# Hybrid decoder step on one core: a credit of 3 for each piece of the sample's state, the memory cache through other tiles, memory values in strips, and another order of the first loads

## The chip, the cores and the metric

One Trainium2 chip, one core. The metric is the device time of one execution in microseconds (us); lower is better. The profile names the engines PE (TensorE, the matrix engine), ACT (ScalarE), DVE (VectorE), POOL (GpSimd) and SP (SyncE, which here only issues transfers). POOL and ACT can issue transfers too. Each engine works through its own instructions in their order.

## The reference

One layer of a decoder for 256 tokens of a prompt and 8 tokens of a sample, all in float32, width 2048:

```python
h = rmsnorm(x); q, k, v, z, xbc, dt, qm, g = split(h @ w_in)
A = sliding-window attention (window 128, ALiBi, sinks; 16 query heads, 4 key heads of 64)
B = Mamba-2 SSD (32 heads of 64, state 128; conv of 4; y * silu(z), group RMSNorm)
M = cross-attention of 4 heads of 256 into 256 memory tokens
x = x + w_out(sig(g0) * w_up_swa(A) + sig(g1) * w_up_ssd(B) + sig(g2) * w_up_mem(M))
x = x + w_down(silu(rmsnorm(x) @ w_gate) * (rmsnorm(x) @ w_up))
```

For the prompt, the memory's keys and values are rmsnorm(mem_prompt) @ w_mem_kv. For each of the 8 sample tokens they come from a cache (`cache_mem_k`, `cache_mem_v`: 256 tokens of 4 heads of 256), and the SSD state comes from `state_ssm` (8 tokens, 32 heads, 64 x 128) and is updated and written out: state = state * decay + B * (dt * x), y = sum(state * C).

## The kernel before

**Weights.** All weight matrices are cut into "units" of 256 x 512 float32 (512 KB), some 610 of them in a fixed order: memory keys and values (units 0 to 31, `pmem`), the input projection (`pin`: memory queries, queries, keys, gates, B, C, dt, x and z by groups), the branch products (`pua` for A, `pum` for M, `pus` for B), `pout`, and the feed-forward part (`pg`, `pu`, `pdn`). SP loads a unit into `raw` four units ahead. ACT writes a rounded copy `hi`, DVE writes the rest `lo = raw - hi` (`split`), three units ahead. PE then does 24 products of 264 columns per unit (12 of 512 in the memory stage): high by high, high by low, low by high. Gate groups of branch B (units 250 to 281) end with unit 281, and the first `pus` is unit 282.

**Side work.** Everything else is written as generators in two lists, `side` and `slow`. After each unit, `step` gives the first of them a credit (1.0 and 0.75, at most 3.0 saved); a generator runs until its yields have spent the credit. The number after `yield` therefore sets how many units pass before the next piece. `drain(name)` runs a task to its end at once. A scheduler then puts the written instructions into each engine's order; it keeps what depends on what and may move the rest.

**The slow list.** `mem_sample_work` (task Mk) multiplies cached keys with queries on DVE (`jks`), `mem_sample_values` (Ms) multiplies the softmax weights with the cached values on PE (`oms`, in strips of 32 rows of the result), then `ssd_sample_work` (Y0 to Y3) updates the state in 32 pieces of 4 tokens and 2 heads: ACT scales (`ring` at L1294), DVE adds and sums (L1295, L1296), POOL writes out. Last comes `ssd_sample_end` (task end): PE sums squares (`ssys`), DVE takes a reciprocal root (L171 to L176) and multiplies (L1316, L1318), ACT and DVE split the result into `sT`, which is an input of every `pus`. `slow.drain("end")` stands in `before_ups(0)`, ahead of unit 282.

**Loads.** `ahead(sources, pool, depth)` issues loads on POOL's queue, `depth` of them before they are used. Tiles come from `lm` (two tiles of 512 KB) or from `ring`, a buffer of two such pieces that is used round and round. The first loads are on SP: memory rows in quarters (`load_mem`), two gain vectors (`vg`), and the first units. PE turns `vg` (`pv`) and the memory rows (`memT`); ACT scales these into `memh` (L316), and the squares of the rows (L327) give their norm.

Of the kernel before, what the change touches and what calls it, by code (L numbers as in the profile page):

```python
# [77 lines left out]
def tile_hybrid_decoder_step(  # L78
# [80 lines left out]
    def mm(out, lhsT, rhs, start=True, stop=True):  # L159
        nc.tensor.matmul(out, lhsT=lhsT, rhs=rhs, start=start, stop=stop)  # L160
# [18 lines left out]
    def split(hi, lo, src):  # L179

        act(hi, src, AF.Copy)  # L181
        V.tensor_tensor(lo, src, hi.bitcast(F32), op=ALU.subtract)  # L182

# [18 lines left out]

    for t in range(2):
        load_mem(t, 0, 0)
    nc.sync.dma_start(vg[0:16], norm_mem[0].rearrange("(c p) -> c p", p=P))
    nc.sync.dma_start(vg[16:32], norm_mix[0].rearrange("(c p) -> c p", p=P))
# [45 lines left out]
    def do_split(n):  # L252
        if n < state["split"]:
            return
        raw = raws.pop(n)
        hi = wp.tile([P, 1024], F32R, tag="hi", name=nm("hi"), bufs=3)
        lo = wp.tile([P, 1024], F32R, tag="lo", name=nm("lo"), bufs=3)
        if units[n].get("perm"):
            for k in range(2):
                v = [t[:, k * 512:(k + 1) * 512].rearrange("p (r a d) -> p a r d", r=4, a=2) for t in (hi, lo)]  # L260
                s = raw[:, k * 512:(k + 1) * 512].rearrange("p (a r d) -> p a r d", a=2, r=4)
                split(v[0], v[1], s)
        else:
            split(hi, lo, raw)
        parts[n] = (hi, lo)
        state["split"] = n + 1
# [53 lines left out]
    def mem_norm():  # L320
        junk = t2("junk", BF16)
        ssm_ = tiny("ssm", 16)
        for h in range(2):
            for t in range(2):
                for c in range(4):
                    o = 8 * t + 4 * h + c
                    act(junk[:, 0:256], mem_t[t, h][:, c * 256:(c + 1) * 256], AF.Square, accum_out=ssm_[:, o:o + 1])  # L327
                yield 1.3
# [9 lines left out]
    def mem_group(cg):  # L338
        st = {}

        def prod(u):
            def f(hi, lo):
                if u == 0:
                    st["ps"] = [dps("pmem") for _ in range(2)]
                if cg == 0:
                    for f in ((0, 1, 2) if u == 0 else (u + 2,)):
# [72 lines left out]
    def prep_x():  # L419
# [4 lines left out]
        for h in range(2):  # L424
            for t in range(2):
# [3 lines left out]
                yield 1.3  # L429
# [165 lines left out]
    mem_loads = ahead([(None, c[0, b, mc * P:(mc + 1) * P].rearrange("m h d -> m (h d)"))  # L595
                       for c in (cache_mem_k, cache_mem_v) for b in range(NS) for mc in range(2)], lm, 2)
# [97 lines left out]
    def mem_sample_work():  # L694
# [3 lines left out]
        for b in range(NS):  # L698
            qb = t4("qb")[:, 0:1024]
            nc.gpsimd.dma_start(qb, qd[b:b + 1].broadcast_to([P, 1024]))  # L700
            for mc in range(2):
                kc = next(mem_loads)
# [23 lines left out]
    def mem_sample_values():  # L726
        pT = mT["p"]
# [12 lines left out]
        o = t1("omsb")[:, 0:256]  # L740
        V.tensor_copy(o, po[:, 0:256])
        ps = sps("omT")
        for d in range(2):
            tr(ps[:, d * P:(d + 1) * P], o[:, d * P:(d + 1) * P])
        o = tiny("omsT", 64)
        V.tensor_copy(o.rearrange("p (h d b) -> p d h b", h=4, d=2),
                      ps[:, 0:256].rearrange("p (d h e) -> p d h e", d=2, h=4)[:, :, :, 0:NS])
# [73 lines left out]
    def swa():  # L821
# [37 lines left out]
        for a in range(2):  # L859
# [6 lines left out]
            yield 1.0  # L866
        qst = [half("qst", F32R) for _ in range(2)]
        for kvp in range(2):
            for a in range(2):
# [5 lines left out]
                yield 0.8  # L875
        for blk in (1, 0):
            nk = 256 if blk else 128
            for kvp in range(2):
# [38 lines left out]
                for rp in range(2):  # L917
                    for kb in range(nk // P):
# [12 lines left out]
                        yield 0.4  # L931
# [348 lines left out]
    def ssd_sample_work(g):  # L1280
# [5 lines left out]
        for j in range(4 * g, 4 * g + 4):  # L1286
# [3 lines left out]
            for b0 in (0, 4):  # L1290
# [7 lines left out]
                yield 2.0  # L1298
# [313 lines left out]
    side.add("x", prep_x())  # L1612
# [63 lines left out]
```

## Time and profile before

| | us |
|---|---|
| median of 3 runs | 1930.85 |
| lowest and highest of them | 1927.42, 1932.12 |
| the profiled execution, device time | 1933.54 |
| its span, first to last instruction | 1931.8 |

| engine | busy us | share of the span |
|---|---|---|
| PE | 1905.2 | 99 % |
| DVE | 1168.0 | 60 % |
| ACT | 969.7 | 50 % |
| POOL | 133.6 | 7 % |

The mean granted clock of PE is 0.999. In the profile a line such as L1294 is a line of the kernel's source; names left and right of the arrow are the tiles that an instruction writes and reads, with buffer numbers left out. In a timeline, a bracket at the end gives the idle time of the engine before the instruction and what ended it; an x8 merges eight of the same kind.

### The profile page before, as it was taken

What the parts mean: (1) busy time and instruction counts of PE and PEld (TensorE: products, weight loads), DVE (VectorE), ACT (ScalarE), POOL (GpSimd) and SP (SyncE); (2) the same over time, 40 slices, a digit from 0 to 9 for tenths busy, and PEclk for the clock granted to TensorE, in tenths of its full rate; (3) what the DMA queues carried; (4) which work ended last, traced back from release to release, by engine and by line L of the source; (5) the groups of instructions that cost most, each with busy time, mean ns of one, the idle gap of its engine ahead of it and who ended that gap; (6) DMA issues with size and microseconds to landing.
All of it is one profiled execution on the core that took longest, in us unless ns stands there. A gap on an engine that the chain in (4) does not pass through costs nothing.

```text
span 1931.8 us, 37682 instructions
## 1 busy us (share of the span) xinstructions
PE 1905.2 (99%) x15401; PEld 1857.1 (96%) x15401; DVE 1168.0 (60%) x2246; ACT 969.7 (50%) x1423; POOL 133.6 (7%) x269
## 2 busy tenths in 40 slices
PE   8999999999999999999999999999999999999998
PEld 6899999989999999999999999999999999999998
DVE  5665577665568878588455666555445555445553
ACT  6654456665657685646444444444334434334443
POOL 3010101001002122011000000000000000000000
PEclk9999999999999999999999999999999999999999
DMA  8686758767668789778656656665556665566653
GB/s 278 209 264 214 212 171 297 223 190 234 200 181 279 241 228 301 250 262 282 180 189 213 222 182 176 184 182 180 183 178 183 178 185 177 184 177 183 176 192 126
DMA packets 191956, 402.92 MB, mean 209 GB/s; under 512 B 13891, under 2 KB 16242, under 8 KB 191648
## 3 DMA queue, kind: packets, MB, share of 16 engines
q1 hardware_dynamic: 169856, 324.13, 54.6%
q0 software_dynamic: 21776, 76.33, 11.9%
q8 instruction: 120, 1.97, 0.4%
q14 instruction: 52, 0.43, 0.1%
q10 hardware_dynamic: 152, 0.07, 0.0%
HBM read 376.53 MB, written 26.22 MB: 208 GB/s over the span
## 4 chain that ended last, share of the span: by engine, by line
PE 87%; DMA 4%; issue 4%; DVE 3%; ACT 2%; POOL 1%; ACTq 0%; SPq 0%; POOLq 0%; DVEq 0%
PE pin L160 25%; PE pu L160 13%; PE pdn L160 13%; PE pg L160 13%; PE pus L160 5%; PE pout L160 5%; PE pmem L160 5%; DMA ring<-in_state_ssm_dram 2%; PE pum L160 1%; PE pua L160 1%; DVE lo L182 1%; DMA ld<-in_cache_mem_v_dram 1%; DVE ring L1295 1%; DMA ld<-in_cache_mem_k_dram 1%; ACT hi L181 0%
## 5 line engine op out<-in xcount | busy, mean ns | idle before, releaser
L182 DVE TENSOR_TENSOR lo<-raw,hi 128x1024 fp32r<-128x1024 f32 (+1 forms) x626 | 746.8, 1196 | 599.4 <-ACT hi L181 598.2
L181 ACT ACTIVATE hi<-raw 128x1024 fp32r<-128x1024 f32 (+1 forms) x626 | 646.0, 1036 | 835.0 <-PE pin L160 191.8
L160 PE MATMUL pin<-hh,hi 128*128 128x264 f32 x1728 | 489.3, 287 | 0.6 <-DVE sig L1439 0.5
L160 PE MATMUL pin<-hl,hi 128*128 128x264 f32 x1728 | 489.0, 286 | 0.0
L160 PE MATMUL pin<-hh,lo 128*128 128x264 f32 x1728 | 473.8, 285 | 1.8 <-DVE lo L182 1.8
L160 PEld LDWEIGHTS pin<-hh,hi 128*128 128x128 f32 x1728 | 325.4, 189 | 5.6 <-issue 3.6
L160 PEld LDWEIGHTS pin<-hl,hi 128*128 128x128 f32 x1728 | 325.5, 188 | 2.7 <-issue 2.4
L160 PEld LDWEIGHTS pin<-hh,lo 128*128 128x128 f32 x1728 | 317.3, 188 | 3.8 <-DVE lo L182 2.3
L160 PE MATMUL pdn<-fah,hi 128*128 128x264 f32 x704 | 199.7, 285 | 0.0
L160 PE MATMUL pdn<-fal,hi 128*128 128x264 f32 x704 | 199.4, 285 | 0.0
L160 PE MATMUL pu<-h2h,hi 128*128 128x264 f32 x704 | 199.4, 284 | 0.0
L160 PE MATMUL pu<-h2l,hi 128*128 128x264 f32 x704 | 199.3, 284 | 0.0
L160 PE MATMUL pg<-h2l,hi 128*128 128x264 f32 x704 | 199.1, 285 | 0.0
L160 PE MATMUL pg<-h2h,hi 128*128 128x264 f32 x704 | 198.4, 284 | 0.0
L160 PE MATMUL pdn<-fah,lo 128*128 128x264 f32 x704 | 197.0, 284 | 0.0
L160 PE MATMUL pu<-h2h,lo 128*128 128x264 f32 x704 | 196.6, 284 | 0.0
L160 PE MATMUL pg<-h2h,lo 128*128 128x264 f32 x704 | 196.1, 284 | 0.0
L160 PEld LDWEIGHTS pdn<-fah,hi 128*128 128x128 f32 x704 | 132.7, 189 | 0.1
L160 PEld LDWEIGHTS pu<-h2h,hi 128*128 128x128 f32 x704 | 132.7, 189 | 0.0
L160 PEld LDWEIGHTS pg<-h2h,hi 128*128 128x128 f32 x704 | 132.7, 188 | 0.0
L160 PEld LDWEIGHTS pdn<-fal,hi 128*128 128x128 f32 x704 | 132.6, 188 | 0.1
L160 PEld LDWEIGHTS pu<-h2l,hi 128*128 128x128 f32 x704 | 132.6, 188 | 0.0
(531 smaller groups left out, 2966.0 us busy)
## 6 DMA issues: line engine op xcount, KB each, us to landing
raw<-in_w_in_dram SPq DMA_DIRECT2D x218, 512.0 KB, 4.3
raw<-in_w_gate_dram SPq DMA_DIRECT2D x88, 512.0 KB, 3.7
raw<-in_w_up_dram SPq DMA_DIRECT2D x88, 512.0 KB, 3.9
raw<-in_w_down_dram SPq DMA_DIRECT2D x88, 512.0 KB, 4.2
raw<-in_w_mem_kv_dram SPq DMA_DIRECT2D x32, 512.0 KB, 4.5
raw<-in_w_up_ssd_dram SPq DMA_DIRECT2D x32, 512.0 KB, 4.2
raw<-in_w_out_dram SPq DMA_DIRECT2D x32, 512.0 KB, 4.4
ld<-in_cache_mem_k_dram POOLq DMA_DIRECT2D x16, 512.0 KB, 5.8
```

Of the source, the lines that this page charges most:

```text
L160: nc.tensor.matmul(out, lhsT=lhsT, rhs=rhs, start=start, stop=stop)
L181: act(hi, src, AF.Copy)
L182: V.tensor_tensor(lo, src, hi.bitcast(F32), op=ALU.subtract)
L1295: V.scalar_tensor_tensor(hb, bb[:, b], dx[:, b:b + 1], hb, op0=ALU.mult, op1=ALU.add)
```

## The change

It has these parts.
1. The two gain loads go from SP's queue to ACT's, ahead of the memory rows. The squares of the memory rows are placed behind ACT's first split. Feature chunks of the memory rows are turned one unit ahead instead of two.
2. The loads of x wait until unit 7 is written, and spend less credit; the sliding-window steps spend less too.
3. The cached keys come through four tiles (`lm` and `ring` in turn), the cached values through `lm` apart from them.
4. The values are multiplied in strips of 32 x 512, four for each token, from one zeroed table of weights; parts are added at the end by four reductions after four transposes.
5. A state piece spends 3.0 instead of 2.0 of credit.

```diff
@@ mem rows, gains
+    nc.scalar.dma_start(vg[0:16], norm_mem[0].rearrange("(c p) -> c p", p=P))
+    nc.scalar.dma_start(vg[16:32], norm_mix[0].rearrange("(c p) -> c p", p=P))
     for t in range(2):
         load_mem(t, 0, 0)
-    nc.sync.dma_start(vg[0:16], norm_mem[0].rearrange("(c p) -> c p", p=P))
-    nc.sync.dma_start(vg[16:32], norm_mix[0].rearrange("(c p) -> c p", p=P))
...
@@ do_split: the first split is kept
-            split(hi, lo, raw)
+            h = split(hi, lo, raw)
+            if n == 0:
+                state["first"] = h
...
@@ mem_norm
-                    act(junk[:, 0:256], mem_t[t, h][:, c * 256:(c + 1) * 256], AF.Square, accum_out=ssm_[:, o:o + 1])
+                    with tc.issue_after(state["first"].ins):
+                        act(junk[:, 0:256], mem_t[t, h][:, c * 256:(c + 1) * 256], AF.Square, accum_out=ssm_[:, o:o + 1])
...
@@ memory units
-                    for f in ((0, 1, 2) if u == 0 else (u + 2,)):
+                    for f in ((0, 1) if u == 0 else (u + 1,)):
...
@@ prep_x, loads of x
-                yield 1.3
+                yield 0.4
...
@@ loads of the caches
-    mem_loads = ahead([(None, c[0, b, mc * P:(mc + 1) * P].rearrange("m h d -> m (h d)"))
-                       for c in (cache_mem_k, cache_mem_v) for b in range(NS) for mc in range(2)], lm, 2)
+    homes = [0]
+
+    def anywhere(name):
+        homes[0] += 1
+        return (lm if homes[0] % 2 else ld)(name)
+
+    memk_loads, memv_loads = (
+        ahead([(None, c[0, b, mc * P:(mc + 1) * P].rearrange("m h d -> m (h d)")) for b in range(NS) for mc in range(2)],
+              pool, depth) for c, pool, depth in ((cache_mem_k, anywhere, 4), (cache_mem_v, lm, 2)))
...
@@ mem_sample_values
-            w = t1("pb")[:, 0:256].rearrange("p (mc h e) -> p mc h e", mc=2, h=4)
-            V.memset(w.rearrange("p mc h e -> p (mc h e)"), 0.0)
-            V.tensor_copy(w[:, :, :, b], pT.rearrange("p (mc b h) -> p mc b h", mc=2, b=NS)[:, :, b])
-            for mc in range(2):
-                vc = next(mem_loads)
-                for h in range(4):
-                    mm(po[32 * h:32 * h + 32, 0:256], w[:, mc, h], vc[:, h * 256:(h + 1) * 256],
-                       start=b == 0 and mc == 0, stop=b == NS - 1 and mc == 1)
-                yield 1.5
...
+        w = t2("pb").rearrange("p (mc b c) -> p mc b c", mc=2, b=NS)
+        V.memset(w.rearrange("p mc b c -> p (mc b c)"), 0.0)
+        for b in range(NS):
+            V.tensor_copy(w[:, :, b, 4 * b:4 * b + 4], pT[:, :, b])
...
+            vc = [next(memv_loads) for _ in range(2)]
+
+            for mc, e in ((1, 0), (1, 1), (0, 0), (0, 1)):
+                o = 64 * mc + 32 * e
+                tc.keep_in_program_order(mm(po[o:o + 32, 0:512], w[:, mc, b], vc[mc][:, 512 * e:512 * e + 512],
+                                            start=b == 0, stop=b == NS - 1))
+            yield 3.0
+        o = t2("omsb")
+        V.tensor_copy(o, po)
...
+        for j in range(4):
+            tr(ps[:, j * P:(j + 1) * P], o[:, j * P:(j + 1) * P])
...
+        for h in range(4):
+            V.tensor_reduce(o.rearrange("p (h d b) -> p h d b", h=4, d=2)[:, h], v[:, h % 2, h // 2, h], axis=AX.X, op=ALU.add)
...
@@ swa_keys, swa: three yields
-            yield 1.0
+            yield 0.3
-                yield 0.8
+                yield 0.3
-                        yield 0.4
+                        yield 0.2
...
@@ ssd_sample_work
-                yield 2.0
+                yield 3.0
...
@@ end of the kernel
-    side.add("x", prep_x())
+    side.add("x", prep_x(), ["go"])
...
         if i == 7:
             side.drain("m")
+            side.ready.add("go")
```

How it moves instructions is shown at three places. First, POOL at the start of the program, before: `knm_bc`, `sink`, `kn_bc`, `dtb_bc` and `na_bc` are small vectors that are copied to all 128 partitions, `vb` and `va` are vectors loaded as rows.

```order
L330 DMA knm_bc<-in_k_norm_mem_dram 128x256
L496 DMA sink<-in_swa_sinks_dram 128x16
masks.py:199 ISA
masks.py:199 AFFINE_SELECT ident<-ident 128x128 [waits Pool_49]
L497 DMA kn_bc<-in_k_norm_swa_dram 128x64
L498 DMA dtb_bc<-in_dt_bias_dram 128x32
L499 DMA na_bc<-in_a_log_dram 128x32
L501 DMA hcol<-in_dt_bias_dram 32x1
L501 DMA hcol<-in_a_log_dram 32x1
L501 DMA hcol<-in_d_skip_dram 32x1
L502 AFFINE_SELECT tri<-ones 128x128 [waits Pool_49]
L513 MEMSET slope 128x1
```

And after:

```order
L221 DMA vb_84<-in_conv_b_dram 24x128
L221 DMA vb_84<-in_ssd_norm_dram 16x128
masks.py:199 ISA
masks.py:199 AFFINE_SELECT ident<-ident 128x128 [waits Pool_49]
L221 DMA vb_84<-in_norm_ffn_dram 16x128
L221 DMA vb_84<-in_q_norm_mem_dram 2x128
L223 DMA vb_84<-in_q_norm_swa_dram 1x16x4 x2
L224 DMA va_83<-in_conv_w_dram 96x128
L334 DMA knm_bc<-in_k_norm_mem_dram 128x256
L500 DMA sink<-in_swa_sinks_dram 128x16 [waits DMASW0_49]
L501 DMA kn_bc<-in_k_norm_swa_dram 128x64 [waits DMASW1_49]
L502 DMA dtb_bc<-in_dt_bias_dram 128x32 [waits DMASW2_49]
```

The rows of `vb` and `va`, seven loads, have moved ahead of the copies to all partitions. On SP, the same place before:

```order
L201 DMA ring<-in_mem_prompt_dram 128x512
L201 DMA mem_87<-in_mem_prompt_dram 128x512
L205 DMA vg_85<-in_norm_mem_dram 16x128
L206 DMA vg_85<-in_norm_mix_dram 16x128
L244 DMA raw_143<-in_w_mem_kv_dram 128x2x512
L201 DMA ring<-in_mem_prompt_dram 128x512
```

And after, where the two `vg` rows stand on ACT's queue and the first `raw` is third:

```order
L202 DMA ring<-in_mem_prompt_dram 128x512
L202 DMA mem_89<-in_mem_prompt_dram 128x512
L245 DMA raw_143<-in_w_mem_kv_dram 128x2x512
L202 DMA ring<-in_mem_prompt_dram 128x512
L202 DMA mem_89<-in_mem_prompt_dram 128x512
L245 DMA raw_145<-in_w_mem_kv_dram 128x2x512
```

Second, PE at the first of the value products (`oms`, read from the cached tiles `ld`), before:

```order
L160 MATMUL ps_4193<-kst_3119,qst_3209 128x128 x8
L160 MATMUL oms_4150<-ld_4255,pb_4343 32x256 x4
L160 MATMUL pin_4269<-hl_115,hi_4315 128x264
L160 MATMUL pin_4269<-hh_113,lo_4316 128x264
L160 MATMUL pin_4269<-hh_113,hi_4315 128x264
L160 MATMUL pin_4269<-hl_115,hi_4315 128x264
L160 MATMUL pin_4269<-hh_113,lo_4316 128x264
L160 MATMUL pin_4270<-hh_113,hi_4315 128x264
L160 MATMUL pin_4270<-hl_115,hi_4315 128x264
L160 MATMUL pin_4270<-hh_113,lo_4316 128x264
L160 MATMUL oms_4150<-ld_4346,pb_4343 32x256 x4
L160 MATMUL pin_4270<-hh_113,hi_4315 128x264
```

And after:

```order
L160 MATMUL pin_4347<-hh_113,lo_4464 128x264
L160 MATMUL pin_4348<-hh_113,hi_4463 128x264
L160 MATMUL oms_4214<-ld_4217,pb_4204 32x512 x2
L160 MATMUL oms_4214<-ld_4215,pb_4204 32x512 x2
L164 MATMUL pT_4256<-ident,s_4000 128x128 x2
L164 MATMUL pT_4256<-ident,s_4001 128x128 x2
L160 MATMUL pin_4348<-hl_115,hi_4463 128x264
L160 MATMUL pin_4348<-hh_113,lo_4464 128x264
```

Two groups of four products of 256 columns, some rows apart, stand there before; one group of four products of 512 columns is there now.

Third, PE at the first `pus` (unit 282), before:

```order
L160 MATMUL pin_11404<-hh_113,hi_11521 128x264
L160 MATMUL pin_11404<-hl_115,hi_11521 128x264
L160 MATMUL pin_11404<-hh_113,lo_11522 128x264
L160 MATMUL pus_11652<-sT_6539,hi_11551 128x264 [waits Activation_49]
L160 MATMUL pus_11652<-sT_6539,hi_11551 128x264
L160 MATMUL pus_11652<-sT_6539,lo_11552 128x264 [waits DVE_49]
```

And after:

```order
L160 MATMUL pin_11258<-hh_113,hi_11392 128x264
L160 MATMUL pin_11258<-hl_115,hi_11392 128x264
L160 MATMUL pin_11258<-hh_113,lo_11393 128x264
L160 MATMUL ssys_11571<-ys_1559_11569,ones 128x32 [waits PE_49]
L160 MATMUL pus_11603<-sT_6301,hi_11422 128x264 [waits Activation_49]
L160 MATMUL pus_11604<-sT_6301,hi_11422 128x264
L160 MATMUL pus_11605<-sT_6301,hi_11422 128x264
```

Before, `ssys` stands nineteen units of products earlier; now it is the row just ahead of the first `pus`, which waits for ACT's `sT`. DVE's rows that lead from `ssys` to `sT` there, after the change:

```order
L182 TENSOR_TENSOR lo_11466<-raw_11420,hi_11465 128x1024 [waits DMAHW6_49,PE_49,Activation_49]
L1330 TENSOR_SCALAR vys_11573<-ssys_11571 128x32 [waits PE_49]
L171 TENSOR_SCALAR rs_y_11575<-vys_11573 128x32 [waits DVE_49]
L172 TENSOR_SCALAR rs_y_11575<-rs_y_11575 128x32 [waits DVE_49]
L174 TENSOR_TENSOR rs_a_11576<-rs_y_11575 128x32 [waits DVE_49]
L182 TENSOR_TENSOR lo_11496<-raw_11463,hi_11495 128x1024 [waits DMAHW7_49,Activation_49]
L175 SCALAR_TENSOR_TENSOR rs_a_11576<-rs_a_11576,vys_11573 128x32 [waits DVE_49]
L176 SCALAR_TENSOR_TENSOR rs_y_11575<-rs_a_11576,rs_y_11575 128x32 [waits DVE_49]
L174 TENSOR_TENSOR rs_a_11576<-rs_y_11575 128x32 [waits DVE_49]
L175 SCALAR_TENSOR_TENSOR rs_a_11576<-rs_a_11576,vys_11573 128x32 [waits DVE_49]
L176 SCALAR_TENSOR_TENSOR rs_y_11575<-rs_a_11576,rs_y_11575 128x32 [waits DVE_49]
L174 TENSOR_TENSOR rs_a_11576<-rs_y_11575 128x32 [waits DVE_49]
```

Before, the same rows stand at the place of `ssys`, nineteen units ahead of the first `pus`; now one `lo` is left among them, and `sT` is read right behind.

More of the change, by code (lines that the diff above doesn't have):

```diff
@@ L159, in mm @@
     def mm(out, lhsT, rhs, start=True, stop=True):
-        nc.tensor.matmul(out, lhsT=lhsT, rhs=rhs, start=start, stop=stop)
+        return nc.tensor.matmul(out, lhsT=lhsT, rhs=rhs, start=start, stop=stop)
     def tr(out, in_):
@@ L179, in split @@
     def split(hi, lo, src):
-        act(hi, src, AF.Copy)
+        h = act(hi, src, AF.Copy)
         V.tensor_tensor(lo, src, hi.bitcast(F32), op=ALU.subtract)
+        return h
     ident = const([P, P], "ident")
@@ L701, in mem_sample_work @@
             for mc in range(2):
-                kc = next(mem_loads)
+                kc = next(memk_loads)
                 jk = t1("jks")
```

9 lines of the change are left out of this document (2 added, 7 removed).

## The prediction

> **What bounds the kernel now.** I read the page's first part, then the busy time by stage, then TensorE's waits, then the timeline around each wait.
>
> ```profile
> PE 1905.2 (99%) x15401; PEld 1857.1 (96%) x15401; DVE 1168.0 (60%) x2246; ACT 969.7 (50%) x1423; POOL 133.6 (7%) x269
> 560.00:760.00 200.00, 192.72 (x1669) 188.65 (x1668) 166.52 (x492) 135.67 (x233) 43.26 (x61) 0.99 0.83 249
> 760.00:876.00 116.00, 115.87 (x1001) 114.71 (x1000) 82.76 (x162) 67.38 (x100) 19.00 (x31) 1.00 0.81 275
> 876.00:1932.00 1056.00, 1050.79 (x8624) 1050.05 (x8623) 565.82 (x777) 441.90 (x511) 8.33 (x13) 1.00 0.60 186
> PE pua L160 <- ACT sig L1434: 3.8, 2, 2.6
> PE pmT L164 <- DVE pm L674: 1.7, 2, 1.3
> ```
>
> The first row is the whole span; the next three are stretches (length, then each engine's busy time and count, TensorE's granted clock, DMA share and GB/s); the last two are waits of TensorE (total us, times, longest). TensorE is busy for 99 % of the 1931.8 us. From 760 us on there is next to nothing to take: 116.00 less 115.87 us idle, and 1056.00 less 1050.79, spread over 8624 matmuls and the end. A gain can come from the start (until the first product, below), from the waits, from 560 to 760 us, where 200.00 less 192.72 leaves 7.3 us idle, and from matmuls that fall away. A loss can come from any new wait of TensorE, above all in the clean part. 0.3 % of the time, 5.8 us, is about what a measurement of this kernel can tell from no change.
>
> **Start: gain loads off SP's queue, POOL's loads in another order.**
>
> ```profile
> 1.73 0.42 SPq L205 DMA_DIRECT2D vg<-in_norm_mem_dram  x1
> 2.66 0.42 SPq L244 DMA_DIRECT2D raw<-in_w_mem_kv_dram  x1
> 1.41 0.72 POOL L330 DMA_DIRECT2D knm_bc<-in_k_norm_mem_dram  x1 [0.25 <-issue]
> 6.91 0.55 POOL L220 DMA_DIRECT2D vb<-in_conv_b_dram  x1 [0.38 <-DMA knm_bc<-in_k_norm_mem_dram]
> 2.00:4.00 2.00, 0.00 (x0) 0.00 (x0) 0.17 (x1) 0.10 (x1) 1.93 (x5) 1.00 0.84 261
> 4.00:7.00 3.00, 0.05 (x1) 0.08 (x1) 0.00 (x0) 1.02 (x4) 2.62 (x8) 1.00 0.92 54
> q0 software_dynamic: 58, 0.10, 84.5%
> q1 hardware_dynamic: 91, 0.06, 7.9%
> 4.08 0.42 ACT L327 ACTIVATE junk<-ring 128x256 bf16<-128x256 f32 x1 [1.99 <-DMA ring<-in_mem_prompt_dram]
> 10.81 1.06 ACT L181 ACTIVATE hi<-raw 128x1024 fp32r<-128x1024 f32 x1 [2.02 <-DMA raw<-in_w_mem_kv_dram]
> 11.61 0.45 PE L164 MATMUL memT<-ident,ring 128*128 128x128 f32 x1 [2.48 <-DMA ring<-in_mem_prompt_dram]
> 11.92 1.22 PE L160 MATMUL pmem<-hi,memh 128*128 128x512 f32 x2
> 17.61 0.27 PE L164 MATMUL memT<-ident,ring 128*128 128x128 f32 x1
> ```
>
> First two issues on SP, then two on POOL (start, duration), two stretches, the share of the 16 DMA engines that POOL's queue q0 and SP's q1 took between 4 and 7 us, and rows of ACT and TensorE. The first product needs the first weights (ACT splits them at 10.81) and the second quarter of a memory row tile (11.61). The DMA engines moved 261 GB/s until 4 us and 54 between 4 and 7. In the poor stretch POOL's small broadcasts (keys' gain, sinks) hold 84.5 % of the engines and SP's queue 7.9 %. SP's weights stand there behind the two gain loads, so its turns go to the gains' small rows. In the changed order the weights follow the first memory quarters (the gains go by ACT's queue), and POOL issues seven small vector loads ahead of the broadcasts, which by the pace of its issues (0.72 and about 0.55 us each) start at some 5.7 instead of 1.41 us. So the 512 KB of weights and 256 KB of rows can flow from 4 us at 261 GB/s, 3.0 us, before the broadcasts come: the first product at some 8 to 9 instead of 11.92. But then the broadcasts fall on the next quarter, for which TensorE waits after two products, and on the second weights. TensorE also works at half speed until 17.61 (0.42 us a product before, 0.23 after), so a start 3.5 us earlier is worth half while that lasts. Bounds: 0 (the same bytes and broadcasts must pass before the second weights) and −4.0; I take the middle, −2.0. The memory squares (4.08) leave idle ACT time and come behind the first split: two of 0.6 us with their read, covered by ACT's 2 us waits there; at most +1.2 without that cover. ACT's two issues take 0.9 us while it waits anyway; the waiting `prep_x` and shorter yields there move side work within a stage that DVE and ACT carry (71 and 68 % at most): 0, ±1.
>
> **Memory keys and values.**
>
> ```profile
> DVE jks L705 <- DMA ld<-in_cache_mem_k_dram: 7.2, 5, 1.9
> L160 PE MATMUL oms<-ld,pb 128*32 128x256 f32 x128 | 10.2, 389 | 1.6 <-DMA ld<-in_cache_mem_v_dram 1.6
> 466.11 1.07 PE L160 MATMUL oms<-ld,pb 128*32 128x256 f32 x16
> 467.11 0.39 PE L160 MATMUL pin<-hh,lo 128*128 128x264 f32 x1
> 487.48 0.64 PE L160 MATMUL oms<-ld,pb 128*32 128x256 f32 x8
> 488.05 0.39 PE L160 MATMUL pin<-hl,hi 128*128 128x264 f32 x1
> 488.28 0.28 PE L160 MATMUL pin<-hh,lo 128*128 128x264 f32 x1
> 476.63 7.49 DMA ld<-in_cache_mem_v_dram
> ```
>
> Four tiles ahead instead of two for the keys' cache: VectorE's five waits (7.2 us) should go, and with them part of TensorE's 1.7 us for `pmT`. Bounds 0 and −1.7; −1.0. What the values cost is read from starts: a group of eight records runs 487.48 to 488.05, 0.57, and the products beside it start 0.1 us late before and after it, together 0.77. Sixteen records in one go take 466.11 to 467.11, 1.00 and 0.2, together 1.2. Before, the 128 records stand in ten single groups and three double ones, 10 × 0.77 + 3 × 1.2 = 11.3 us. After, they stand in eight groups of the same column work (32 × 512 four times instead of 32 × 256 eight times), 8 × 1.2 = 9.6. The gain is 1.7, less 0.2 for two more transposes at the end: −1.5. Bounds: +6 if strips twice as wide ran one after another (each group then twice 1.0), −4 if the shorter records alone count. I take the row of sixteen, since it is the same work in strips. The copies and reductions added on VectorE (four of 32 columns each) lie beside products.
>
> The value loads now wait for the whole group before, and both tiles come at once. Landing took 7.49 us for the load of the 1.6 us wait. The gaps between groups, at 2.92 us a unit (24 products of 1050.79/8624 = 0.122, by the last of the stretches), are 6.7 us at the smallest, once, then 7.7 and more; the pair lands 0.5 to 1 us after the single one. That is one wait of about 1.1 instead of 1.6: −0.5. Bounds −1.6 (no wait) and +1.5 (two waits).
>
> **State pieces every fourth unit.**
>
> ```profile
> ACT ring L1294 <- DMA ring<-in_state_ssm_dram: 18.9, 12, 3.4
> 742.78 10.45 DMA ring<-in_state_ssm_dram
> 753.25 0.69 ACT L1294 ACTIVATE ring<-ring,dsc 128x128 f32<-128x128 f32 x2 [2.88 <-DMA ring<-in_state_ssm_dram]
> 754.27 0.39 PE L160 MATMUL pua<-aTh,hi 128*128 128x264 f32 x1 [2.62 <-ACT sig L1434]
> 754.86 0.42 PE L160 MATMUL pua<-aTh,hi 128*128 128x264 f32 x1
> 758.34 0.29 PE L160 MATMUL pua<-aTh,hi 128*128 128x264 f32 x1
> ```
>
> ACT scales each state piece (`ring`) in its order, and 12 times its transfer is not there. At 753.25 that holds the gate's copies behind it, and TensorE stands for 2.62 us until 754.27. After it the products are 0.42 us long until 758, then 0.29, as in the first stretch of half speed: 3.4 us at half speed, 1.7 lost. With the 7.3 us idle of this stretch about 9 us hang on it. A piece every 4 units instead of 2.67 spreads the loads and VectorE's work, and the loads stand earlier before their use by a few instructions; but the piece still waits in ACT's order, and a transfer of 10.45 us is longer than three units. Bounds: −9.0, and +4.3 (one more wait of 2.6 with its 1.7); the middle is −2.4. In the changed order I find six places, against the twelve waits, where a load is used within about three units of its issue; so half of the 9 goes, −4.5, which I take.
>
> **The end of the state work, now at the drain.** This is the loss. The 32 pieces at the slower pace don't fit before the branch products; the drain writes the end of it between the last `pin` of unit 281 and the first `pus`.
>
> ```profile
> 905.74 0.31 PE L160 MATMUL ssys<-ys,ones 128*128 128x32 f32 x2
> 906.09 0.19 DVE L1313 TENSOR_SCALAR vys<-ssys 128x32 f32<-128x32 f32 x1 [0.84 <-PE ssys L160]
> 906.96 1.23 DVE L182 TENSOR_TENSOR lo<-raw,hi 128x1024 fp32r<-128x1024 f32 x1
> 908.10 0.19 DVE L175 SCALAR_TENSOR_TENSOR rs_a<-rs_a,vys 128x32 f32<-128x32 f32 x1
> 911.27 0.19 DVE L176 SCALAR_TENSOR_TENSOR rs_y<-rs_a,rs_y 128x32 f32<-128x32 f32 x1
> 912.02 0.29 DVE L1318 TENSOR_TENSOR ysd<-ysd,vbc 128x128 f32<-128x128 f32 x1
> 912.86 0.57 ACT L181 ACTIVATE sT<-ysd 128x32 fp32r<-128x32 f32 x4
> ```
>
> From the sum product to VectorE 0.35 us, four small steps to 906.96 0.87, one split's lower half to 908.10 1.14, seven small steps of 0.225 and the last (1.8 together), four multiplications from 911.49 to 912.02 0.53, one more 0.29, and the first of ScalarE's four copies, 0.15 to 0.2: 5.2 us. Before, nineteen units of products hid it. After, `pus` stands right behind `ssys` on TensorE, nothing between. Then the half clock, by the row at 754.27: 3.4 us of it, 1.7. Together +6.9; bounds +4.1 (no split between, no slow clock) and +8.5 (a second split between, 1.14, and a little more clock).
>
> [...]
>
> **Sum.** −2.0 −1.5 −1.0 −0.5 −4.5 +6.9 = −2.6 us on an execution of 1933.5 us (span 1931.8 and 1.7 around it), which stands 2.7 above the median of the runs, 1930.85. On the median: 1928.3.
>
> **Rivals.**
> Faster: no state piece waits any more (−9.0), the start gives 4.0: −2.6 −4.5 −2.0 = −9.1, 1921.8. For it: 12 waits with a mean of 1.6 us are short. Against it: state tiles are as many as before.
> The change doesn't bring its loss: the chain at the drain is hidden, −2.6 −6.9 = −9.5, 1921.4. Nothing in the order of TensorE speaks for it.
> Slower: in the state stretch one more piece is late by a wait such as that of 754.27, 2.6 + 1.7, and none of the others goes: −2.6 +4.5 +4.3 = +6.2, 1937.0. It decides from the point where a load lands later than ScalarE reaches it with a gate's copy behind it; 10.45 us of landing against 11.7 us of four units leaves 1.2.
> The start does nothing, since the broadcasts only move onto other loads: 1930.3.
> No half clock after the drain, since the clock does not fall for every gap (the row of 560 to 760 us has 0.99 with 7.3 us idle in it): −2.6 −1.7, 1926.6.
> [...]
>
> **Numbers.** Forecast 0.40 (own range 1925 to 1931); no gain at the start 0.13; no half clock 0.10; all state waits gone 0.20; chain hidden 0.05; one more late piece 0.12. The two fast cases lie more than 5.8 us below the median, 0.25, and 0.05 comes from the low tails of the others: faster 0.30. The late piece stands at the edge of 5.8 us above it, and most of its chance goes there: slower 0.10. Same 0.60. Range 1919 to 1936.
>
> **What would show it.** Right: TensorE waits for ScalarE's `sT` some 5 us at the first `pus`, half-speed products behind it; the first `pmem` at 8 to 10 us; eight groups of `oms` with about 1.2 us each; fewer waits of `ring` for its transfers. Wrong: an idle time in 560 to 760 us as large as 7.3, wide strips that take 2 us a group, or a first product at 11 to 12 us. The forecast fails low if the state waits vanish and high if the chain is longer than its rows.

## The result, and the profile after

The changed kernel takes 1945.91 us (median of 5 runs, 1944.25 to 1948.92), the kernel before, run beside it, 1930.85: 15.1 us more, ratio 1.0080 (95 % interval 1.0059 to 1.0101). The forecast was 1928.3, at most 1936. The profiled execution has a span of 1943.0 us, 11.2 more than the one before.

The page's first part, and the stages that answer to those of before (length, busy time and count of PE, PEld, DVE, ACT and POOL, clock, DMA share, GB/s):

```profile
PE 1907.1 (98%) x15339; PEld 1857.6 (96%) x15339; DVE 1169.7 (60%) x2242; ACT 967.0 (50%) x1421; POOL 133.6 (7%) x269
0.00:12.00 12.00, 5.72 (x19) 4.52 (x20) 3.90 (x11) 5.77 (x14) 8.98 (x23) 1.00 0.79 243
560.00:760.00 200.00, 190.88 (x1632) 187.08 (x1631) 145.84 (x388) 125.39 (x207) 30.91 (x44) 0.99 0.78 230
760.00:876.00 116.00, 110.30 (x942) 108.02 (x941) 86.11 (x181) 67.17 (x103) 21.94 (x35) 1.00 0.82 273
876.00:1943.00 1067.00, 1057.02 (x8665) 1056.21 (x8663) 572.31 (x813) 446.09 (x523) 13.73 (x21) 1.00 0.61 186
```

PE's own work is the same (1907 against 1905 us). What grew is idle time: 9.1 us from 560 to 760 (7.3 before), 5.7 from 760 to 876 (0.1 before), 10.0 behind it (5.2 before). The stretch that was clean before is not clean any more. Of PE's waits (us in total, times, longest), those that matter here:

```profile
PE pin L160 <- ACT hi L181: 6.7, 4, 2.1
PE pus L160 <- ACT sT L181: 4.9, 1, 4.9
PE pin L160 <- DVE lo L182: 3.7, 4, 1.7
PE pua L160 <- ACT sig L1451: 1.9, 2, 1.6
PE xtok L164 <- ACT xs L1054: 1.8, 1, 1.8
PE pum L160 <- DVE sig L1438: 1.5, 1, 1.5
PE pmT L164 <- DVE pm L686: 0.2, 1, 0.2
```

The wait for `sT` was forecast. The waits for `hi`, `lo`, `xs` and the gates' `sig` are those of an ACT and a DVE that come late. One thing that can hold ACT is a state piece that has not landed; the row of ACT's waits for state pieces read 18.9, 12, 3.4 before:

```profile
ACT ring L1311 <- DMA ring<-in_state_ssm_dram: 37.5, 12, 4.3
```

One such place in the timeline, POOL's issue first, then ACT, then PE:

```profile
648.20 0.75 POOL L595 DMA_DIRECT2D ring<-in_state_ssm_dram  x1
653.16 1.28 ACT L1311 ACTIVATE ring<-ring,dsc 128x128 f32<-128x128 f32 x4 [3.91 <-DMA ring<-in_state_ssm_dram]
654.34 1.04 ACT L181 ACTIVATE hi<-raw 128x1024 fp32r<-128x1024 f32 x1
655.43 0.39 PE L160 MATMUL pin<-hh,hi 128*128 128x264 f32 x1 [2.05 <-ACT hi L181]
```

The load of a piece is issued at 648.20. ACT reaches the piece and stands for 3.91 us until it has landed, scales it, and only then makes the `hi` that PE has wanted for 2.05 us. It is not the only such place. Between 500 us and the first `pus` PE has eleven waits of over 0.3 us, 16.2 us together. Seven of them, 10.0 us, end within 9 us of the moment at which ACT got a piece it had stood for, and at six of the seven ACT works without a break from that piece to the result that PE waits for. In the kernel before there are seven waits, 7.6 us together, and three of them, 4.7 us, are of this kind.

### The profile page after: what moved, and what is told of

It reads as the page before. It is cut to its first block, busy times and chain, and to the rows that moved or that the text cites. A ratio compares the mean times of both kernels' runs of the same rounds, so it can differ in the third digit from the quotient of the medians.

```text
span 1943.0 us, 37550 instructions
## 1 busy us (share of the span) xinstructions
PE 1907.1 (98%) x15339; PEld 1857.6 (96%) x15339; DVE 1169.7 (60%) x2242; ACT 967.0 (50%) x1421; POOL 133.6 (7%) x269
## 4 chain that ended last, share of the span: by engine, by line
PE 59%; DMA 2%; issue 1%; DVE 1%; ACT 1%; POOL 0%; ACTq 0%; POOLq 0%; DVEq 0%
PE pu L160 13%; PE pdn L160 13%; PE pg L160 13%; PE pin L160 7%; PE pus L160 5%; PE pout L160 5%; DMA ring<-in_state_ssm_dram 1%; PE pum L160 1%; PE pua L160 1%; DMA bb<-bc_d 0%; DMA mgi<-mg_d 0%; DVE lo L182 0%; PE yt L164 0%; ACT hi L181 0%; DVE ring L1312 0%
## 5 line engine op out<-in xcount | busy, mean ns | idle before, releaser
L160 PE MATMUL pin<-hh,lo 128*128 128x264 f32 x1728 | 480.8, 287 | 3.8 <-DVE lo L182 3.7
```

The lines of the kernel that those rows point to most:

```text
L160: return nc.tensor.matmul(out, lhsT=lhsT, rhs=rhs, start=start, stop=stop)
```

## The experiments

"Before" in each is the kernel before, run beside it; the medians of its runs lie between 1929.5 and 1931.4 us.

**Which part costs.** Twelve kernels take parts away from the changed kernel or put them on the kernel before.

```diff
 # a_no_state: the changed kernel
-                yield 3.0
+                yield 2.0
 # b_state: the kernel before
-                yield 2.0
+                yield 3.0
```

> The changed kernel with the state pieces' credit back at 2.0 (all other parts kept). Theory 1: that credit carries the whole loss, both the chain from ssys to sT at the first pus and the new waits of 500 to 960 us (hi and the gate copies late behind ring on ACT). Then the wait of pus for sT is gone, the idle time of PE from 560 to 760 us falls back to 7 us or less, and the time is 1926 to 1930 us. Theory 2: the credit brings only the chain at pus (6.5 us); the new waits of the state stretch come from the other parts, which move side work against the state pieces. Then the time is 1937 to 1940 us.

> The kernel before with the credit of 3.0 for a state piece alone. Theory 1 (the credit carries the whole loss): 1941 to 1945 us, with a wait of about 5 us of pus for sT and half speed behind it, and several new waits of PE from 560 to 900 us. Theory 2 (only the chain at pus): 1936 to 1938 us.

Measured: a_no_state 1929.94 us, ratio to before 0.9999 (0.9987 to 1.0011); b_state 1937.52, 1.0040 (1.0026 to 1.0054). The credit of 3.0 is in all of the loss, but it costs 7 us alone and 16 in the changed kernel. Each theory is right for one of the two kernels.

```diff
 # b_start: the kernel before with part 1 (both gain loads on ACT, issue_after, feature chunks)
+    nc.scalar.dma_start(vg[0:16], ...)
-                    for f in ((0, 1, 2) if u == 0 else (u + 2,)):
+                    for f in ((0, 1) if u == 0 else (u + 1,)):
 # b_mem: the kernel before with parts 3 and 4 (memk_loads, memv_loads, strips)
```

> The kernel before with part 1 alone: gains on ACT's queue, squares behind the first split, feature chunks one unit ahead. Both theories: the first pmem at 8.5 to 9 us instead of 11.92, about 2 to 3 us gained, 1927.5 to 1929 us. Rival: POOL's order and not the queue of the gains lets the first weights through; then it is seen whether POOL's vector loads stand ahead of the broadcasts here too, and the first pmem stays near 11 us if they don't.

> The kernel before with parts 3 and 4 alone: keys through four tiles, values in strips of 32 x 512. By the prediction about 3 us gained, 1928 us (pmT does not wait, eight groups of oms at 1.2 us). Rival: the strips or the longer gaps between loads cost what they save, and the wait of 2.1 us for hi at 505 us (with 1.7 us of half speed behind it) comes from these parts: 1930 to 1934 us.

Measured: b_start 1931.40, 1.0009 (0.9993 to 1.0024); b_mem 1929.77, 1.0000 (0.9987 to 1.0013). Neither moves the time by itself. In b_start PE's first rows after a wait are these:

```profile
8.40 0.45 PE L164 MATMUL memT<-ident,ring 128*128 128x128 f32 x1 [1.09 <-DMA ring<-in_mem_prompt_dram]
19.77 0.33 PE L164 MATMUL memT<-ident,mem 128*128 128x128 f32 x1 [2.57 <-DMA mem<-in_mem_prompt_dram]
```

The early product is there (the second quarter of the rows at 8.40, 11.61 before), and POOL's vector loads stand ahead of the broadcasts here too; but then PE waits 2.57 us for the other rows, and nothing is left.

```diff
 # a_end262: the changed kernel
+        if i == 262:
+            side.drain("N3")
+            slow.drain("end")
 # a_credit25: the changed kernel
-                yield 3.0
+                yield 2.5
 # a_no_swa: the changed kernel, yields of swa_keys and swa as before (1.0, 0.8, 0.4)
 # a_no_mem: the changed kernel without parts 3 and 4
```

> The changed kernel with the end of the state work (side's N3, then slow's end) drained at unit 262 instead of 282; the credit of 3.0 stays until there. This prices the chain at the first pus by itself. If the chain and its half speed cost what their rows in the trace say (5.2 + 1.7 or more), the time falls by 6 to 9 us, from 1945.9 to about 1938, and the new waits of the state stretch, some 8 us, are left. Rival: the chain costs nothing by itself, because what is late there is late anyway: 1944 or more. A second rival: the pieces drained at once crowd ACT and DVE around 262 and bring a new wait of 2 us or more.

> The changed kernel with a credit of 2.5 for a state piece. Its ssys stands some twelve units ahead of pus. Theory A (a slower pace itself puts pieces against the gate copies and the memory branch): the chain is hidden, but part of the waits in the state stretch stays: 1934 to 1938. Theory B (it is the drain and what it crowds): 1929 to 1931, as with 2.0.

> The changed kernel with the three shorter yields of the sliding-window steps undone. The credit of 3.0 alone cost 7 us on the kernel before, but 16 in the changed one. Theory A: the shorter yields bring the side work (gates, chunks, conv) forward against the state pieces, so undoing them leaves the loss of the credit alone, 1937 to 1939. Theory B: they have no part in it, 1944 to 1948.

> The changed kernel with the old key loads and value products (parts 3 and 4 undone). Theory A: the value strips with their credit of 3.0 shift the start of the state pieces, and only with them does the slower pace cost 16 us; undone, 1937 to 1939. Theory B: no part in it, 1944 to 1948 (by the medians of the memory parts alone, which moved nothing).

Measured: a_end262 1938.38, 1.0042 (1.0024 to 1.0060), so the chain at the first `pus` costs some 7.5 us (the two intervals allow 2 to 13; the changed kernel was run five times). a_credit25 1934.04, 1.0019 (1.0005 to 1.0032): the chain is hidden, some of the rest stays. a_no_swa 1936.03, 1.0028 (1.0016 to 1.0040): the shorter yields cost 9.9 us in the changed kernel. a_no_mem 1952.93, 1.0111 (1.0090 to 1.0132): both theories missed; without the new key and value parts the changed kernel is 7 us longer still, though the intervals of the two (1.0059 to 1.0101 with them) overlap a little.

```diff
 # b_swa: the kernel before with the shorter yields of swa_keys and swa alone
 # a_no_state_swa: the changed kernel, credit 2.0 and the old yields there
 # a_no_swa_end262: a_no_swa with the drain at unit 262
 # a_swa_po_only: the changed kernel, of the three yields only the 0.2 kept
```

> The kernel before with the three shorter yields of the sliding-window steps alone. If they harm by themselves: 1933 to 1936, with ACT's wait for state loads near 28 us instead of 18.9 and a new wait of PE for hi at some 505 us. If only together with the slower pieces: 1930 to 1931.

> The changed kernel without its two parts on pace (credit 2.0, old yields of the sliding-window steps): start, memory rows, x behind the eighth unit, keys and values remain. If the shorter yields harm only together with the slower pieces, as with all other parts and credit 2.0: 1929 to 1930. If they harm by themselves (ACT's waits for state loads were 27.6 us with them and credit 2.0, 19 us in the memory parts alone): 1924 to 1927, and ACT's waits for state loads near 19 us.

> The changed kernel with the old yields of the sliding-window steps and the state's end drained at unit 262; the credit of 3.0 stays until there. If the two losses add, 1936.0 less 7.5 (the price of the chain measured by draining at 262): 1928 to 1929. If the pieces drained at 262 crowd the stretch in this order, 1931 or more.

> The changed kernel with two of the three shorter yields of the sliding-window steps undone (keys and query copies back at 1.0 and 0.8; the step after each product stays at 0.2). The three together cost 10 us with credit 3.0 and nothing with 2.0. If what counts is how early the chunk work begins against the state pieces, a part of the shortening gives a part or all of the 10 us: 1938 to 1946, with the new waits at the same units (186, 190, 218 to 220, 250) if all of it. If only the early steps matter: 1936.

Measured: b_swa 1930.79, 0.9999 (0.9990 to 1.0009); a_no_state_swa 1930.90, 1.0000 (0.9990 to 1.0010); a_no_swa_end262 1929.83, 0.9997 (0.9988 to 1.0007); a_swa_po_only 1945.76, 1.0076 (1.0060 to 1.0092). The shorter yields harm only together with the slower pieces, and the smallest of them (0.4 to 0.2) is enough, though its new waits lie at other units (162 to 174, 214) than expected. Without chain and yields nothing is lost, and nothing is won.

**What the pieces cost.** Who waits, and for what?

```diff
 # a_pool: the changed kernel
-                    act(hb, hb, AF.Copy, scale=ssd["dsc"][:, j, 8 + b:9 + b])
+                    nc.gpsimd.tensor_scalar(hb, hb, ssd["dsc"][:, j, 8 + b:9 + b], None, op0=ALU.mult)
```

> The changed kernel with the scaling of the state pieces on POOL instead of ACT, all else kept. Theory: the extra loss, some 8 us beside the chain at pus, comes from ACT, which stands 37.5 us (18.9 before) at state loads that are not there, with the splits and gate copies queued behind it. With the wait on POOL, ACT does not wait, PE's waits for hi, xs and sig from 560 to 900 us go, and the time falls from 1945.9 to 1936 to 1939, the chain at pus being left. Rival: the pieces collide with DVE's work or with the DMA traffic, whoever scales them: 1943 or more. POOL's own pieces are as long as ACT's or longer, so that pieces may also end later.

Measured: 1946.68, 1.0082 (1.0067 to 1.0097). The theory fell in this form. The rows of waits show why: POOL now waits 45.0 us for the loads, DVE waits for POOL in its place, and PE for DVE's `lo` instead of ACT's `hi`. The pieces take longer on POOL: from 560 to 760 us it is busy for 91.1 us with 107 instructions, 30.9 with 44 in the changed kernel, which makes, as an estimate, 1.0 us for each one more; on ACT the changed kernel's 128 have a median of 0.39 us.

```profile
POOL ring L1311 <- DMA ring<-in_state_ssm_dram: 45.0, 14, 7.8
DVE ring L1312 <- POOL ring L1311: 12.0, 8, 4.6
PE pin L160 <- DVE lo L182: 6.0, 5, 2.3
```

```diff
 # a_noload: the changed kernel; b_noload: the kernel before
+            if n < 4:
+                nc.gpsimd.dma_start(held[n]..., srcs[n])
+            yield held[n % 4]
 # a_scratch: the changed kernel; three tiles held, the other 29 loads into a fourth that nothing reads
+            if n + 3 < 32:
+                nc.gpsimd.dma_start(held[3]..., srcs[n + 3])
+            yield held[n % 3]
 # a_far: the changed kernel; four tiles held, the other loads go memory to memory
+            with tc.issue_after(wrote[-1]) if wrote else ExitStack():
+                nc.gpsimd.dma_start(far[n + 4], srcs[n + 4])
```

> The changed kernel in which only the first four state pieces are loaded; the other 28 use the four tiles again without a load (28 of 32 state loads are left out, so the state's numbers are not the reference's). ACT and DVE do the same work and every piece is written out. Theory: the extra loss beside the chain at pus comes from state loads that land late, whichever engine waits for them (scaled on POOL, the wait stood before DVE's lower halves instead of ACT's). Then ACT's 37.5 us of waits for state loads go, and the time falls to 1934 to 1939, the chain at pus being left. Rival: the pieces' work itself crowds ACT and DVE between gates, chunks and the memory branch, loaded or not: 1943 or more.

> The changed kernel in which three state pieces are loaded and used again and again, and the other 29 loads land in a fourth tile that nothing reads (the state's numbers are not the reference's). The DMA traffic stays, only the wait for it is gone. If lateness is the cause: as without the loads, 1934 to 1939. If it is the traffic, which delays weights and other small loads: 1942 or more here, with a gain only in the kernel without the loads.

> The changed kernel in which four state pieces are loaded and used again; the other 28 loads are issued on POOL behind the write of the piece before, at the same places, but go from memory to memory where nobody waits for them (the state's numbers are not the reference's). The traffic of the loads stays, the wait for their landing is gone. If lateness is the cause: as without the loads, 1929 to 1933. If the traffic (which delays weights, small vectors and writes) has a part in it: 1936 or more.

> The kernel before in which four state pieces are loaded and used again, the other 28 loads left out (the state's numbers are not the reference's). It prices the late state loads where they stood before the change: ACT waited 18.9 us for them there, 37.5 in the changed kernel, and leaving them out of that one took 16 us. In proportion 8 us: 1922 to 1924. If they were hidden before: 1929 to 1931.

Measured: a_noload 1929.64, 0.9995 (0.9984 to 1.0007); a_scratch 1960.20, 1.0151 (1.0135 to 1.0167); a_far 1929.87, 1.0002 (0.9990 to 1.0013); b_noload 1924.86, 0.9976 (0.9965 to 0.9987). a_far has as many transfers and no wait for their landing, and is as short as a_noload: the traffic alone does not cost the 16 us, and what goes with the wait for the landing does. Its seven waits of PE over 0.3 us between 500 us and the chain are 6.2 us together, and none of them stands behind a piece that had not landed. The comparison is not perfectly clean. The transfers of a_far start a median of 26 us ahead of the piece's use, those of the changed kernel 7, and some 120 of ACT's 1421 rows stand in another order. Nor is ACT free of waits at the pieces: a held tile is used again, and in a_far ACT stands for DVE's sums on it. In b_noload it stands for sums and for writes:

```profile
ACT ring L1324 <- DVE s L1326: 22.9, 18, 2.5
ACT ring L1302 <- DMA out_dram<-ring: 11.9, 4, 5.6
ACT ring L1302 <- DVE s L1304: 8.5, 8, 2.3
```

So the total of ACT's waits is no price; it matters what stands behind each. a_scratch says nothing on the traffic. Each of its loads waits on POOL for the one before to land in the same tile, with the writes behind it, and one write held ACT for 21.0 us and PE for 14.9:

```profile
ACT ring L1322 <- DMA out_dram<-ring: 26.7, 5, 21.0
PE pin L160 <- ACT hi L181: 22.0, 4, 14.9
```

The stage of 560 to 760 us shows the same in a_far and in b_noload, PE's busy time second:

```profile
560.00:760.00 200.00, 196.23 (x1692) 192.64 (x1691) 155.21 (x418) 134.77 (x227) 35.90 (x51) 1.00 0.79 247
560.00:760.00 200.00, 197.49 (x1724) 193.43 (x1724) 170.15 (x502) 144.65 (x253) 27.52 (x41) 1.00 0.77 232
```

By these medians late state loads cost 1945.9 − 1929.9 = 16.0 us after the change and 1930.3 − 1924.9 = 5.5 before, the first uncertain by some 5 us and the second by some 2.

```diff
 # b_half: the kernel before, pieces of two tokens in eight tiles of 256, credit 1.0 each
-                         for j in range(16) for b in (0, 4)], lambda _: piece(512), 4)
+                         for j in range(16) for b in (0, 2, 4, 6)], lambda _: piece(256), 8)
```

> The kernel before with state pieces of half the size: two tokens instead of four, eight tiles of 256 instead of four of 512 in the same buffer, a credit of 1.0 each, so that all the work is the same and the pace too. If lateness of the loads comes from tiles that are freed late, seven of eight tiles can be on their way while one is worked on, instead of three of four, and the 5.5 us that the late loads cost before shrink to 0 to 3: 1925 to 1929. Rival: what is late is the queue on POOL and the transfer itself; twice as many loads and writes then wait as long each, or longer: 1930 or more.

Measured: 1930.69, 1.0008 (0.9999 to 1.0017). ACT still waits:

```profile
ACT ring L1294 <- DMA ring<-in_state_ssm_dram: 24.7, 17, 4.0
```

Smaller pieces in the same buffer don't help. No version with all of the work beats the kernel before. Whether more tiles would help was not tried.

## Why the prediction was wrong

**The state stretch is the step that failed.** The prediction took −4.5 us for pieces "every 4 units instead of 2.67", with +4.3 as its upper end. In the two profiled executions PE takes 7.5 us more from its first `pua` to the last product ahead of the first `pus` (571.2 to 965.7 us, before 574.3 to 961.4). Measured by leaving the loads out, late state loads rose from 5.5 to 16.0 us: +10.5. Of the 9 us that the step saw hanging on late pieces before, leaving the loads out gave 5.5.

Two things in that step were wrong. First, the credit does not set the distance between pieces in ACT's order. Four units are 11.7 us, but from the trace after, the fifth to eighth piece are scaled at 568.0, 574.6, 581.5 and 587.9 us; before, the same four at 587.6, 593.3, 599.8 and 601.9. The credit moves the order in which work is written, and so which work stands behind a piece in ACT's and DVE's rows. Second, the step took the distance of a load to its use in that order for slack. The load itself is issued late, when a tile has come free and POOL has got to it (POOL stands 69.6 us for DVE's sums ahead of these loads, 51.7 before), and ACT uses most pieces as soon as they have landed: issued at 641.2, landed at 646.0 and scaled from 646.1; then 656.2, 660.4, 660.7; then 661.0, 667.1, 667.2. Over the 28 pieces behind the first four the median from issue to use is 7.3 us before and 6.4 after, and 5.9 and 5.8 of that pass until the landing. The slower credit gave no more lead. The 10.45 us by which the step reckoned was the longest landing of the 32, and their median is 5.5 in both kernels.

**The yields of the sliding-window steps** have no term of their own; "shorter yields" stand with `prep_x` at 0, ±1. Alone they are worth that (b_swa). With the slower pieces they cost 9.9 us. The prediction priced parts one by one, and this price belongs to two parts together. Parts 3 and 4 may be another case: worth 0 alone, they save 7 us in the changed kernel, by intervals that overlap.

**The chain at the first `pus` was right.** Its rows, PE, DVE, PE:

```profile
965.74 0.30 PE L160 MATMUL ssys<-ys,ones 128*128 128x32 f32 x2
966.91 1.23 DVE L182 TENSOR_TENSOR lo<-raw,hi 128x1024 fp32r<-128x1024 f32 x1
970.39 0.29 DVE L1335 TENSOR_TENSOR ysd<-ysd,vbc 128x128 f32<-128x128 f32 x1
971.00 1.47 PE L160 MATMUL pus<-sT,hi 128*128 128x264 f32 x5 [4.95 <-ACT sT L181]
974.02 0.42 PE L160 MATMUL pus<-sT,lo 128*128 128x264 f32 x1
974.43 0.28 PE L160 MATMUL pus<-sT,lo 128*128 128x264 f32 x1
```

From `ssys` to the first `pus` 5.26 us (5.2 summed), one `lo` within it, then half speed (0.42 us a product) until 974.4, 3.4 us. From the first `pus` to the end the profiled execution takes 972.0 us instead of 970.4, so that wait and half speed are 5.3 and 1.6, together 6.9 as forecast. Its price by a_end262 is 7.5 us, and by a_no_swa less a_no_swa_end262 it is 6.2. That half speed lasted only 3.4 us there was partly luck: after the same wait the products stay at half speed for 5.9 us in b_state (964.51 to 970.40) and for some 5.7 in a_no_swa (960.60 to 966.3). The gap of 4.95 us is followed by half speed, as the row at 754.27 of the kernel before had it. So are two shorter ones of the changed kernel: after PE's waits of 2.12 us until 505.64 and 2.05 us until 655.43 the granted clock is 0.5, from 506.75 to 510.16 and from 656.93 to 660.34.

**The start was right in mechanism, too large in worth.**

```profile
4.00:7.00 3.00, 1.58 (x8) 1.55 (x9) 0.19 (x1) 0.99 (x1) 2.59 (x5) 1.00 1.05 334
q1 hardware_dynamic: 521, 0.98, 102.0%
8.46 0.45 PE L164 MATMUL memT<-ident,ring 128*128 128x128 f32 x1 [0.86 <-DMA ring<-in_mem_prompt_dram]
8.78 1.22 PE L160 MATMUL pmem<-hi,memh 128*128 128x512 f32 x2
13.41 0.27 PE L164 MATMUL memT<-ident,ring 128*128 128x128 f32 x1
18.18 0.33 PE L164 MATMUL memT<-ident,mem 128*128 128x128 f32 x1 [1.18 <-DMA mem<-in_mem_prompt_dram]
```

From 4 to 7 us 334 GB/s moved instead of 54, 0.98 of the 1.00 MB on SP's queue, and the first product came at 8.78 (forecast 8 to 9, 11.92 before); full speed was granted from 11.8 us on instead of 17.3. Then PE waits 1.18 us for the next rows, as the step warned. At the first product of unit 32 the trace has 1.7 us left of 3.1 (110.86 against 112.60 us).

**Keys and values were right in the trace.** `pmT` waits 0.2 us (1.7 before, −1.5 where −1.0 was taken), no value load is waited for, and eight records of 512 columns take 0.99 us, from 462.15 to 463.14, as the row of sixteen said:

```profile
462.15 1.06 PE L160 MATMUL oms<-ld,pb 128*32 128x512 f32 x8
463.14 0.66 PE L164 MATMUL Btok<-ident,BT 128*128 128x128 f32 x4
```

**The sum again.** The two profiled executions can be compared at PE's first `pua`, at its last product ahead of the first `pus`, at the first `pus` and at the end. The time to the first `pua` falls by 3.2 us (571.16 against 574.32), where −5.0 was forecast for the start, the keys and the values; the state stretch takes 7.5 more, where −4.5 was forecast; the chain takes 6.9. That is 11.2, the difference of the two spans. Part of what the −3.2 lacks is a new wait that no step named:

```profile
505.64 0.39 PE L160 MATMUL pin<-hh,hi 128*128 128x264 f32 x1 [2.12 <-ACT hi L181]
```

ACT scales three pieces there in one go ahead of this `hi`. They had landed by 465 us, so this is no late load, and a_far and a_noload keep the wait. With the half speed behind it, 1.7 us of loss, it is worth some 3.8 us in this execution.

The medians are 15.1 us apart and not 11.2, since the profiled execution before was 2.7 above its median and the one after 1.2 below. Much of this is clock. The five executions of the changed kernel have a mean granted clock of 0.9952 (the profiled one 0.997, the highest), the 23 executions of the kernel before that were run beside a_far 0.9986. The missing share of the time is 9.3 us in the one and 2.7 in the other. By this estimate some 6 to 7 of the 15.1 us are half speed behind the waits and the chain, and not the waits themselves.

By leaving parts out: chain +7.5 and late state loads +10.5 are 18.0, and the −2.9 to the 15.1 measured is what is left for the rest. a_far against b_noload, both without late loads, gives 5.0 = 7.5 − 2.5 for the same, where −5.0 was forecast. These differences are each uncertain by 3 to 5 us. The small gains don't show in kernels that keep the state loads (b_start, b_mem and a_no_state_swa within 0.2 % of before); that the waits for state pieces take them back is likely, and not shown.

Why the slower pieces and the shorter yields together bring the pieces into a worse place, and each alone does not, stays open. The length of ACT's waits for state loads does not tell it: 37.5 us in the changed kernel, 28.7 in b_state, 27.2 in b_swa, 29.4 in a_no_swa and 29.8 in a_swa_po_only. Yet b_swa is as long as before, the 7 us of b_state are the chain's (from the first `pua` to the last product ahead of `pus` it takes no longer than before), and a_swa_po_only is as long as the changed kernel.

The slower rival was the nearest to the truth: its mechanism, a late piece with a gate's copy behind it, took place at several units, not at one. It had a chance of 0.12 and gave 1937.0, above the end of the stated range. Of the prediction's signs of being wrong one came, the idle time of 9.1 us from 560 to 760, and of its signs of being right the fewer waits of `ring` did not: they are twelve again, and twice as long.

## What to carry to other kernels

Where side work is placed by credits, a changed number is not a changed pace: look up in the trace when each piece really runs and what it waits for, and price the wait by leaving the load out, since a wait that is hidden in one order is not in the next. An engine that makes an input of the bound engine in its own order of work (here ACT and DVE with `hi` and `lo`) is a bad place to wait for a late transfer: by the medians, leaving the late loads out saved 16.0 us after the change and 5.5 before it. Moving that wait to POOL did not help (1946.68 us against 1945.91), since DVE then waited 12.0 us for POOL. A task that is drained ahead of its first use needs its own length in slack there: 5.2 us of small steps and the half speed behind them were some 7 us.

## What the runs showed of the hardware

Between the first full speed (from 11.8 us on, 17.3 before) and 1940 us, the clock records of the changed kernel hold three stretches at a granted clock of 0.5: from 506.75 to 510.16, from 656.93 to 660.34 and from 970.96 to 974.37 us, 3.41 us each. Those of the kernel before hold one, from 754.59 to 758.00 us, behind PE's waits of 0.83 us until 750.15 and 2.62 us until 754.27. Not every wait is followed by one: from 660.35 to 970.95 us the clock of the changed kernel is 1.00, and of the waits of PE that end there the longest is 1.83 us (until 671.86). Nor is a gap of the same length always followed by the same time at half speed. In b_state, with the same 4.95 us wait, the products stay at half speed until 970.4, 5.9 us, where the changed kernel has 3.4:

```profile
959.26 0.30 PE L160 MATMUL ssys<-ys,ones 128*128 128x32 f32 x2
964.51 1.47 PE L160 MATMUL pus<-sT,hi 128*128 128x264 f32 x5 [4.95 <-ACT sT L181]
970.57 0.41 PE L160 MATMUL pus<-sT,hi 128*128 128x264 f32 x2
```

Why the same wait is followed by 3.4 us at half speed in the one run and by 5.9 in the other is not shown.

From 4 to 7 us before, POOL's queue, mostly small broadcasts, held 84.5 % of the DMA engines with 0.1 MB, and SP's queue, on which the gain loads issued at 1.73 and 2.20 us took 4.9 and 4.6 us to land, 7.9 % with 0.06 MB; with the broadcasts later and the gains on another queue, the engines moved six times as much in these 3 us. That the broadcasts are slow by themselves is not shown: while they are on their way in the changed kernel, from 7 to 11 us, POOL's queue takes 20.1 % with 0.19 MB, and 321 GB/s pass in all.
